# A macaron layer on one core: other holds, another order into the attention, and new homes and order for the output projection

## The chip, the cores and the metric

The kernel runs on 1 core of one Trainium2 chip. The metric is the time of one execution on the device in microseconds (us), lower is better. The engines are named as in the profile: PE (TensorE, matmuls), PEld (its weight loads), ACT (ScalarE), DVE (VectorE), POOL (GpSimd), and SP, whose queue issues all the DMAs spoken of here. Each engine runs its instructions in program order; they wait for each other by semaphores.

## The reference

One layer on x of 1024 tokens by 1024 features, all in float32: a half SwiGLU network, stick-breaking attention with 16 heads of 64, and a second half SwiGLU network with an inner width of 2816.

```
x = x + 0.5 * swiglu(rms_norm(x, g1), w1_in, w1_out)
x = x + attention(rms_norm(x, gm), w_qkv, gq, gk, w_o)
x = x + 0.5 * swiglu(rms_norm(x, g2), w2_in, w2_out)

swiglu(y, w_in, w_out):  gate, up = split(y @ w_in);  (silu(gate) * up) @ w_out
attention:  q, k = rms_norm per head;  z = q k^T / 8;  only keys s < t
            w[t, s] = sigmoid(z[t, s]) * product over s < j < t of (1 - sigmoid(z[t, j]))
            concat(w @ v) @ w_o
```

## The kernel before, in words

Every product is made of three matmuls (L271, L272, L273): an operand is split by `split` (L179: ACT writes a rounded high part; L180: POOL or DVE subtracts it to get the low part), and high x high, low x high and high x low are added up in one PSUM bank. So each operand costs one ACT and one DVE or POOL instruction before PE can use it. In the profile the tiles have the names of the program: `wqh`/`wql` are the parts of the q, k, v weights, `xh`/`xl` those of the normed input, `th`/`tl` those of a turned block of attention weights, `rp` and `u` those of weights on their way into the two networks.

The first network runs to about 672 us. Its second product, `ffn_out`, is made of seven products in the manner of Strassen (`SEVEN`), called m = 5, 1, 4, 3, 7, 2, 6 in this order; each runs over six chunks of the inner width and leaves its result in four banks `ma` or `mb`, which DVE adds to x with a factor of plus or minus a half (L557). A caller's function `at` is called behind chunks, blocks and products, and puts work of the next stage there: sums of squares (L214, ACT), the norm's rates (L188 to L195, many tiny DVE instructions), the scaled rows `xs` (L234, DVE) and their turning on PE into `xh`, `xl`.

The attention goes over eight pairs of heads, p = 0 to 7, one every 67 us, up to 1263 us. In a pair PE makes the scores of blocks (L817, `bz<-kh_s,q_s`), ACT, DVE (a scan, L823) and POOL (a product and a memset, L830 and L828) make the weights `w` from them, PE turns these (L852, `bt<-ident,w`), ACT and DVE split them into `th` and `tl`, and PE applies them to the values (L870, `bo<-th,vst` and `bo<-tl,vst`). Scores alone would leave PE waiting, so the q, k, v product of the next pair (`bq<-wqh,xh`) is cut into steps and laid between. The order is written out in a plan: a pair has parts a, b, c, d with spans (`PARTS`), every step is put at a time of its part (`put`), and the steps are issued sorted by that time. When a row block of q, k, v is finished (L739 to L751), ACT makes squares and copies, DVE the values' low part `vst` (L744), and after four blocks the norm's rates `r` (L751) and `f` (L762), and POOL scales `qk` (L755, L758).

The weights of the pair after next are fetched by `weights_of` in four steps (`LOADS`). So that the ACT conversion (L707) isn't scheduled too early, a tiny POOL instruction first writes one element of each weight tile's place from `qk`: a hold (L706), on which the conversion then depends.

Outputs of pairs are stored to DRAM (L884) and loaded back as rows of `xh` and `xl` (L895). The output projection is in two halves of columns. Its first half's weights are fetched in four pieces `wo0` to `wo3` of two pairs each (L987) and split, the low parts on POOL (`ON_POOL`). Its products for the first seven pairs are laid into the last pair as filler (`SHARES`, 8 places; `project`, L1000 adds to x); the eighth pair's products for all eight row blocks come when the attention has ended. Then the second half runs. `first_weights` fetches the second network's first weights into a ring of 18 tiles `u`, beginning at number 0. All loads and stores stand on SP's one queue, in program order.

Of the kernel before, what the change touches and what calls it, by code (L numbers as in the profile page):

```python
# [34 lines left out]
ON_POOL = {"wo0", "wo1", "wo2", "wo3"}  # L35
# [12 lines left out]
SHARES = (("b", 6.0), ("b", 11.0), ("c", 3.0), ("c", 9.0), ("c", 15.0), ("d", 1.5), ("d", 5.0), ("d", 8.5))  # L48
# [44 lines left out]
SHARE = 7  # L93
# [10 lines left out]
def macaron_kernel(ctx, tc, x, g1, w1_in, w1_out, gm, w_qkv, gq, gk, w_o, g2, w2_in, w2_out, out):  # L104
# [67 lines left out]
    above = cpool.tile([P, 112], F32, name="above")  # L172
# [53 lines left out]
    def norm(pl, row, tbs, gain, ss=None, r=None):  # L226
# [4 lines left out]
        for i, tb in enumerate(tbs):  # L231
            xs = pl["xs"].tile([P, D], F32, name="xs")
            for h in range(2):
                dve.scalar_tensor_tensor(  # L234
                    out=xs[:, HALVES[h]], in0=row(tb, h), scalar=r[:, i : i + 1], in1=gain[:, HALVES[h]],
                    op0=ALU.mult, op1=ALU.mult,
                )
# [97 lines left out]
    def first_weights(pl, raws, behind=None):  # L335

        place["u"] = place["h"] = 0
# [6 lines left out]
    def first_pair(pl, us, turns):  # L344
# [6 lines left out]
        for t, c in ((0, T0), (1, T1)):  # L351
# [14 lines left out]
            for j in range(2):  # L366
                h = small(pl, "h")
                g = pl[f"h{place['h'] + 3}"].tile([P, NHALF], F32, name="h", bufs=1)
# [129 lines left out]
    def ffn_out(pl, w_out, keep, x_from, ahead, at):  # L498
# [25 lines left out]

        open_banks = {}
        loaded = set()
        for m, tag, fresh, goes in SEVEN:
            last = m == SEVEN[-1][0]
            if fresh:
# [18 lines left out]

            n = len(CHUNKS) - BY_BLOCK if last else len(CHUNKS)
            for c in range(n):  # L550
                add(range(4), [c])
                at(x_sb, m, c)
            for t in range(4):
                add([t], range(n, len(CHUNKS)))
                for (th, h), sign in goes:
                    xc = x_sb[h][:, 4 * (1 - th) + t, :]
                    dve.scalar_tensor_tensor(  # L557
                        out=xc, in0=bs[t], scalar=0.5 * sign, in1=xc, op0=ALU.mult, op1=ALU.add
                    )
                if last:  # L560
                    at(x_sb, m, f"block {t}")
            at(x_sb, m, "end")
# [26 lines left out]
    with pools(*RAWS) as pr:  # L589
# [41 lines left out]
        with banks("ps2"), pools(*SECOND) as pl:  # L631
# [4 lines left out]
            def at(x_sb, m, where):  # L636
# [19 lines left out]
                elif (m, where) == (6, 0):  # L656
                    pending.extend(norm(pn, row, (6, 7), gain_m, r=late.pop()))
# [12 lines left out]
            ffn_out(pl | pr, w1_out, keep, x, ops, at)  # L670
# [3 lines left out]

    marks = []
    with ExitStack() as stack:
# [9 lines left out]
        def weights_of(p, state, behind=None):  # L686
# [6 lines left out]
            def step(n, k):  # L693
# [10 lines left out]
                if behind:  # L704
                    there = behind[n]()
# [392 lines left out]
```

## Time and profile before

| what | value |
|---|---|
| time, median of 3 runs | 1969.98 us (1968.36 to 1972.76) |
| the profiled execution's own time | 1967.96 us |
| its span in the trace | 1966.2 us |
| mean granted PE clock | 0.997 |
| busy PE, PEld | 1917.2 us (98%), 1641.7 us (83%) |
| busy DVE, POOL, ACT | 1248.8 us (64%), 1086.9 us (55%), 983.4 us (50%) |
| DMA | 260.25 MB, mean 132 GB/s |

A row of a timeline gives start and duration in us, engine, line, operation, the tiles written and read, and how often; in brackets stands the idle time of the engine just before it and what ended that. Two instructions of a kind in a row can stand in one row with their common time. A row of PE's waits gives the total idle time in us, how often, and the longest. A row of the windows gives for each stretch the busy time of PE, PEld, DVE, ACT and POOL with the count of instructions, then the granted PE clock, the share of DMA time and GB/s.

### The profile page before, as it was taken

What the parts mean: (1) busy time and instruction counts of PE and PEld (TensorE: products, weight loads), DVE (VectorE), ACT (ScalarE), POOL (GpSimd) and SP (SyncE); (2) the same over time, 40 slices, a digit from 0 to 9 for tenths busy, and PEclk for the clock granted to TensorE, in tenths of its full rate; (3) what the DMA queues carried; (4) which work ended last, traced back from release to release, by engine and by line L of the source; (5) the groups of instructions that cost most, each with busy time, mean ns of one, the idle gap of its engine ahead of it and who ended that gap; (6) DMA issues with size and microseconds to landing.
All of it is one profiled execution on the core that took longest, in us unless ns stands there. A gap on an engine that the chain in (4) does not pass through costs nothing.

```text
span 1966.2 us, 27322 instructions
## 1 busy us (share of the span) xinstructions
PE 1917.2 (98%) x9656; PEld 1641.7 (83%) x9656; DVE 1248.8 (64%) x1823; ACT 983.4 (50%) x1802; POOL 1086.9 (55%) x957
## 2 busy tenths in 40 slices
PE   7999999999999899999999999999999999999999
PEld 7978888888888798898889897789888888888887
DVE  7855545536767667877787778474645644547644
ACT  6533433443335467777777776344343343343332
POOL 3667666656445445555655645113666666755454
PEclk9999999999999999999999999999999999999999
DMA  5223323238996311111111234411332332359984
GB/s 209 86 93 122 106 88 120 95 123 287 355 321 222 105 33 44 38 39 44 36 37 42 66 103 164 166 60 54 118 102 100 121 102 86 124 195 350 317 274 148
DMA packets 168504, 260.25 MB, mean 132 GB/s; under 512 B 11568, under 2 KB 81200, under 8 KB 168368
## 3 DMA queue, kind: packets, MB, share of 16 engines
q1 hardware_dynamic: 168368, 258.52, 38.3%
q8 instruction: 75, 1.23, 0.3%
q14 instruction: 61, 0.50, 0.1%
HBM read 198.18 MB, written 60.29 MB: 131 GB/s over the span
## 4 chain that ended last, share of the span: by engine, by line
PE 79%; DVE 9%; POOL 4%; ACT 4%; issue 3%; DMA 1%; SPq 0%; ACTq 0%; DVEq 0%; POOLq 0%
PE ka L271 6%; PE ka L272 6%; PE ka L273 6%; PE kc L273 4%; PE kc L272 4%; PE kc L271 4%; PE kb L272 4%; PE kb L273 4%; PE kb L271 4%; PE bq L271 3%; PE bq L272 3%; PE bq L273 3%; PE ma L271 3%; PE ma L272 3%; PE ma L273 3%
## 5 line engine op out<-in xcount | busy, mean ns | idle before, releaser
L180 POOL TENSOR_TENSOR rp<-raw,rp 128x1024 fp32r<-128x1024 f32 x84 | 205.8, 2453 | 189.7 <-ACT rp L179 174.5
L180 POOL TENSOR_TENSOR u<-sf,u 128x512 fp32r<-128x512 f32 x160 | 225.9, 1413 | 152.3 <-ACT u L179 148.4
L180 POOL TENSOR_TENSOR u<-raw,u 128x512 fp32r<-128x512 f32 x136 | 195.8, 1445 | 173.4 <-ACT u L179 172.4
L830 POOL TENSOR_TENSOR w<-w,om 128x512 f32<-128x512 f32 (+4 forms) x128 | 142.4, 1115 | 120.0 <-DVE om L823 93.6
L179 ACT ACTIVATE u<-sf 128x512 fp32r<-128x512 f32 x160 | 100.7, 630 | 215.3 <-PE kb L272 86.8
L390 DVE TENSOR_TENSOR h<-h 128x512 f32<-128x512 f32 x110 | 135.3, 1235 | 88.6 <-POOL h L494 87.9
L271 PE MATMUL bq<-wqh,xh 128*128 128x384 f32 x512 | 174.6, 341 | 2.1 <-DVE vst L744 2.1
L179 ACT ACTIVATE rp<-rh 128x1024 fp32r<-128x1024 f32 (+1 forms) x78 | 76.5, 984 | 198.4 <-issue 65.4
L273 PE MATMUL bq<-wqh,xl 128*128 128x384 f32 x512 | 172.2, 336 | 0.0
L272 PE MATMUL bq<-wql,xh 128*128 128x384 f32 x512 | 172.1, 336 | 0.0
L271 PE MATMUL ka<-xh,u 128*128 128x512 f32 (+1 forms) x448 | 162.2, 362 | 1.9 <-ACT s L442 1.4
L179 ACT ACTIVATE u<-raw 128x512 fp32r<-128x512 f32 x136 | 85.0, 632 | 154.9 <-PE ka L272 101.3
L272 PE MATMUL ka<-xl,u 128*128 128x512 f32 (+1 forms) x448 | 161.9, 361 | 0.0
L273 PE MATMUL ka<-xh,u 128*128 128x512 f32 (+1 forms) x448 | 161.6, 361 | 0.0
L515 DVE TENSOR_TENSOR raw<-raw 128x1024 f32<-128x1024 f32 (+1 forms) x60 | 86.4, 1445 | 96.4 <-DMA raw<-w_out 76.4
L273 PE MATMUL ma<-rp 128*128 128x512 f32 x352 | 137.6, 391 | 3.6 <-DVE rp L180 3.6
L271 PE MATMUL ma<-rp 128*128 128x512 f32 x352 | 137.9, 392 | 0.1
L272 PE MATMUL ma<-rp 128*128 128x512 f32 x352 | 137.6, 391 | 0.0
L821 ACT ACTIVATE w<-bz,f 128x512 f32<-128x512 f32 (+1 forms) x192 | 112.8, 587 | 46.2 <-PE bz L817 40.6
L494 POOL TENSOR_TENSOR h<-h,g 128x512 f32<-128x512 f32 x80 | 112.5, 1406 | 32.7 <-DVE h L446 32.7
L419 DVE TENSOR_TENSOR sf<-raw 128x512 f32<-128x512 f32 x80 | 80.2, 1003 | 78.0 <-POOL u L180 78.0
L180 DVE TENSOR_TENSOR rp<-rh,rp 128x1024 fp32r<-128x1024 f32 (+1 forms) x70 | 110.0, 1590 | 19.2 <-ACT rp L179 16.7
(253 smaller groups left out, 5550.1 us busy)
## 6 DMA issues: line engine op xcount, KB each, us to landing
raw<-w_out SPq DMA_DIRECT2D x120, 512.0 KB, 5.7
raw<-w_in SPq DMA_DIRECT2D x88, 512.0 KB, 3.5
k<-h SPq DMA_DIRECT2D x154, 256.0 KB, 2.1
rh<-k SPq DMA_DIRECT2D x64, 512.0 KB, 6.0
raw_qkv<-w_qkv SPq DMA_DIRECT2D x64, 192.0 KB, 2.9
x_keep<-x SPq DMA_DIRECT2D x32, 256.0 KB, 2.9
x<-x_keep SPq DMA_DIRECT2D x32, 256.0 KB, 5.0
raw<-w_out SPq DMA_DIRECT2D x24, 256.0 KB, 4.2
```

The lines of the kernel that those rows point to most:

```text
L179: act.activation(hi, raw, AF.Copy)
L180: (engine or dve).tensor_tensor(lo, raw, hi.bitcast(F32), op=ALU.subtract)
L271: pe.matmul(dst, ah, bh, start=start and i == 0, stop=False, skip_group_check=onto)
L272: pe.matmul(dst, ah, bl, start=False, stop=False, skip_group_check=onto)
L273: pe.matmul(dst, al, bh, start=False, stop=stop and i == n - 1, skip_group_check=onto)
L390: dve.tensor_tensor(src, hb[of[0]], hb[of[1]], op=getattr(ALU, of[2]))
L419: dve.tensor_tensor(f[n], x, y, op=op)
L494: pool_e.tensor_tensor(h, h, gs[k], op=ALU.mult)
L515: dve.tensor_tensor(w[0], w[0], w[1], op=getattr(ALU, W_OF[m][2]))
L821: act.activation(to, z, AF.Sigmoid, scale=state["f", half][:, sign, tb % 4, hd : hd + 1])
L830: pool_e.tensor_tensor(wt[:, c1 : c0 + n], wt[:, c1 : c0 + n], om[:, c1 - 1 : c0 + n - 1], op=ALU.mult)
```

## The change

Three parts.

Holds. The hold in front of a weight conversion is now written by an engine and into a part that are named for each step. For the first two of a pair's four steps two DVE instructions write two elements each into the high part, from the rates `r`; the POOL hold from `qk` goes into the low part. For the last two steps POOL writes the high part as before. The first pair's last two steps wait for the last block of `xl`.

The order into the attention. In the first `ffn_out`, the results of m = 2 are no longer added when its products end but by `finish_late`, with a factor that is read from a tile `signs`; that tile is first written from the low part of chunk 2 of m = 6, so everything on it stands behind that split. The norm of rows 6 and 7 gets the same hold on each `xs`.

The output projection. `wo3`'s low part moves from POOL to DVE; the pieces get other rooms; the low parts of `wo0` and `wo1` wait for two notes (`seen`), taken from the last pair's `qk` and `k`, and the high part of `wo2` for the low part of `wo1`. The places of the filler change: row block 6 gets all eight pairs in one go, the eighth pair of row blocks 4 and 5 goes into part d, and row block 7 stands whole at the very end of the attention; four row blocks' eighth pair is left for afterwards. The ring of `u` tiles begins at number 8.

```diff
-ON_POOL = {"wo0", "wo1", "wo2", "wo3"}
+ON_POOL = {"wo0", "wo1", "wo2"}
...
-SHARES = (("b", 6.0), ("b", 11.0), ("c", 3.0), ("c", 9.0), ("c", 15.0), ("d", 1.5), ("d", 5.0), ("d", 8.5))
+SHARES = (
+    (("b", 6.0), 4, (0, 7)), (("b", 11.0), 5, (0, 7)), (("c", 3.0), 0, (0, 7)), (("c", 9.0), 1, (0, 7)),
+    (("c", 15.0), 6, (0, 8)), (("d", 1.5), 2, (0, 7)), (("d", 5.0), 3, (0, 7)), (("d", 8.5), 4, (7, 8)),
+    (("d", 12.5), 5, (7, 8)), (("d", 17.0), 7, (0, 8)),
+)
...
-PROJECTION = ("wa", "x0", "wb", "wc", "we", "wf", "wg", "wd", "wh", "wi", "wj", "wk", "wl", "x1")
-WO_FIRST = ("raw2", "raw3", "raw4", "raw5", "wa", "wb", "wd", "wc")
+PROJECTION = ("wa", "wb", "wc", "wd", "x0", "we", "wf", "wg", "wh", "wi", "wj", "wk", "wl", "x1")
+WO_FIRST = ("raw2", "raw3", "raw4", "raw5", "wa", "wd", "wb", "wc")
...
-    def norm(pl, row, tbs, gain, ss=None, r=None):
+    def norm(pl, row, tbs, gain, ss=None, r=None, behind=None):
...
+            if behind is not None:
+                dve.tensor_scalar(xs[:, 0:1], behind, 1.0, None, op0=ALU.mult)
...
-        place["u"] = place["h"] = 0
+        place["u"], place["h"] = at, at // 2 % H_TILES
...
+        def finish_late(m, goes, result, signs, ops):
+            for i, (_, sign) in enumerate(goes):
+                dve.memset(signs[:, i : i + 1], 0.5 * sign)
+            for t in range(4):
+                result(t, signs)
+            at(x_sb, m, "end", ops)
...
+            late = held is not None and m == SEVEN[-2][0]
...
+            def result(t, scales=None, bs=bs, goes=goes):
+                for i, ((th, h), sign) in enumerate(goes):
+                    xc = x_sb[h][:, 4 * (1 - th) + t, :]
+                    by = 0.5 * sign if scales is None else scales[:, i : i + 1]
+                    dve.scalar_tensor_tensor(out=xc, in0=bs[t], scalar=by, in1=xc, op0=ALU.mult, op1=ALU.add)
+
+            if last and held is not None:
+
+                there = ops[held][1][1][:, 0, 0:1].bitcast(F32)
+                signs = cpool.tile([P, 2], F32, name="signs")
+                dve.tensor_scalar(signs, there.to_broadcast([P, 2]), 1.0, None, op0=ALU.mult)
+                late_result(signs, ops)
...
-                if behind:
-                    there = behind[n]()
-                    pool_e.tensor_tensor(h_[:, k % 4, 0:1], there, there, op=ALU.mult)
+                for engine, to, f in behind[n]:
+                    there = f().to_broadcast([P, 2])
+                    engine.tensor_tensor((h_, l_)[to][:, ks, 0], there, there, op=ALU.mult)
...
-                held = (lambda s=nxt: s["qk", 1][:, 0, 4, 0:1], lambda s=nxt: s["qk", 0][:, 2, 0, 0:1])
+                held = (
+                    ((dve, 0, lambda s=nxt: s["r"][:, 0, 0:1]), (pool_e, 1, lambda s=nxt: s["qk", 1][:, 0, 4, 0:1])),
+                    ((pool_e, 0, lambda s=nxt: s["qk", 0][:, 2, 0, 0:1]),),
+                )
...
+                def note(i, f):
+                    pool_e.tensor_tensor(seen[:, i : i + 1], f(), f(), op=ALU.mult)
+
+                put("c", 14.0, partial(note, 0, lambda s=nxt: s["qk", 1][:, 0, 4, 0:1]))
+                put("d", 1.0, partial(note, 1, lambda s=nxt: s["k", 0, 1][1][:, 0:1].bitcast(F32)))
...
+            if c is HALVES[0] and k < 6:
+
+                there = seen[:, k // 2 : k // 2 + 1] if k < 4 else wo[-1][1][:, 0:1].bitcast(F32)
+                pool_e.tensor_tensor((l_ if k < 4 else h_)[:, 0:1], there, there, op=ALU.mult)
...
-        for i, tb in enumerate(ORDER):
+        for i, (_, tb, pairs) in enumerate(SHARES):
             with as_at(marks[1 + i]):
-                project(tb, range(SHARE), 0, EARLY)
+
+                project(tb, range(*pairs), 0, EARLY if i + 1 < len(SHARES) else ("bt",))
...
-        for tb in ORDER:
-            project(tb, range(SHARE, NP), 0, ROUND)
+        for tb in ORDER[4:]:
+            project(tb, range(NP - 1, NP), 0, ROUND)
...
-        hb = first_pair(pa | pr, first_weights(pa | pr, ahead), {(0, 3): turn_rest})
+        hb = first_pair(pa | pr, first_weights(pa | pr, ahead, at=8), {(0, 3): turn_rest})
```

The change shifts line numbers: L180 becomes L183, L242 is the former L234, L570 the former L557, L783 the former L751, L794 the former L762, L855 the former L823, L908 the former L876, L1047 the former L1000.

DVE in a steady pair, where the rates `r` and `f` of four row blocks are made and a `tl` follows; before:

```order
L823 SCALAR_TENSOR_TENSOR om<-bz,om,first 128x512
L194 TENSOR_TENSOR rs_u<-rs_u,bq 128x16
L195 SCALAR_TENSOR_TENSOR bq<-rs_u,bq 128x16
L751 TENSOR_SCALAR r<-bq 128x4x2
L762 TENSOR_SCALAR f_7945<-bq 128x8 x2
L180 TENSOR_TENSOR tl<-bt,th 128x512
L823 SCALAR_TENSOR_TENSOR om<-bz,first 128x256
```

And now:

```order
L855 SCALAR_TENSOR_TENSOR om<-bz,om,first 128x512
L197 TENSOR_TENSOR rs_u<-rs_u,bq 128x16
L198 SCALAR_TENSOR_TENSOR bq<-rs_u,bq 128x16
L783 TENSOR_SCALAR r<-bq 128x4x2
L794 TENSOR_SCALAR f_7956<-bq 128x8 x2
L738 TENSOR_TENSOR wqh<-r 128x2 x2
L183 TENSOR_TENSOR tl<-bt,th 128x512
L855 SCALAR_TENSOR_TENSOR om<-bz,first 128x256
```

Two holds (L738) stand between the rates and `tl`.

DVE on the way into the attention, in the last products of the first network; `raw` are sums of weights (L515, now L524), `mb` the banks of m = 2; before:

```order
L234 SCALAR_TENSOR_TENSOR xs<-x_4340,rs_y,gain 128x512
L234 SCALAR_TENSOR_TENSOR xs<-x_4341,rs_y,gain 128x512
L515 TENSOR_TENSOR raw<-raw 128x1024 x2
L557 SCALAR_TENSOR_TENSOR x_4340<-mb_5525,x_4340 128x512
L557 SCALAR_TENSOR_TENSOR x_4341<-mb_5525,x_4341 128x512
L557 SCALAR_TENSOR_TENSOR x_4340<-mb_5526,x_4340 128x512
L557 SCALAR_TENSOR_TENSOR x_4341<-mb_5526,x_4341 128x512
L557 SCALAR_TENSOR_TENSOR x_4340<-mb_5527,x_4340 128x512
L557 SCALAR_TENSOR_TENSOR x_4341<-mb_5527,x_4341 128x512
L557 SCALAR_TENSOR_TENSOR x_4340<-mb_5528,x_4340 128x512
L557 SCALAR_TENSOR_TENSOR x_4341<-mb_5528,x_4341 128x512
L180 TENSOR_TENSOR rp<-rh,rp 128x1024
```

And now:

```order
L242 SCALAR_TENSOR_TENSOR xs<-x_4341,rs_y,gain 128x512
L524 TENSOR_TENSOR raw<-raw 128x1024 x2
L183 TENSOR_TENSOR rp<-rh,rp 128x1024
L576 TENSOR_SCALAR signs<-rp 128x2
L240 TENSOR_SCALAR xs<-rp 128x1 x2
L536 MEMSET signs 128x1 x2
L242 SCALAR_TENSOR_TENSOR xs<-x_4340,rs_y,gain 128x512
L570 SCALAR_TENSOR_TENSOR x_4340<-mb_5525,signs,x_4340 128x512
L570 SCALAR_TENSOR_TENSOR x_4341<-mb_5525,signs,x_4341 128x512
L524 TENSOR_TENSOR raw<-raw 128x512
```

The split `rp` comes ahead of the results and of three of the four halves of `xs`, and three small writes stand behind it.

DVE in the last pair, behind the update of the output tile `o1`; `w12`, `w13` and `om` are scans over blocks, `wf` a split of the projection's second half, `x0` the sum with the projection; before:

```order
L780 SCALAR_TENSOR_TENSOR kl_s0_12683<-bz_12684,gk_sb_6223,kh_s0_12682 128x512
L876 TENSOR_TENSOR o1_12678<-bo_12679,o1_12678 64x512
L823 SCALAR_TENSOR_TENSOR w13_12702<-bz_12703,first_6511 128x128
L823 SCALAR_TENSOR_TENSOR om_12718<-bz_12719,first_6511 128x512
L1000 TENSOR_TENSOR x0_13207<-bq_13241,x0_13207 128x512
L823 SCALAR_TENSOR_TENSOR om_12718<-bz_12727,om_12718,first_6511 128x512
```

And now:

```order
L812 SCALAR_TENSOR_TENSOR kl_s0_12706<-bz_12707,gk_sb_6230,kh_s0_12705 128x512
L908 TENSOR_TENSOR o1_12701<-bo_12702,o1_12701 64x512
L183 TENSOR_TENSOR wf_13500<-raw_13497,we_13499 128x1024
L1047 TENSOR_TENSOR x0_13230<-bq_13267,x0_13230 128x512
L855 SCALAR_TENSOR_TENSOR om_12741<-bz_12742,first_6520 128x512
L855 SCALAR_TENSOR_TENSOR w12_12692<-bz_12693,first_6520 128x256
L855 SCALAR_TENSOR_TENSOR w13_12725<-bz_12726,first_6520 128x128
```

The split `wf`, the sum `x0` and the scan `om` now stand ahead of the scans `w12` and `w13`; `w12` stood ahead of `kl_s0` before.

More of the change, by code (lines that the diff above doesn't have):

```diff
@@ L551, in ffn_out @@
                 add(range(4), [c])
-                at(x_sb, m, c)
+                at(x_sb, m, c, ops)
             for t in range(4):
                 add([t], range(n, len(CHUNKS)))
[L555 to L559, printed above, removed]
-                if last:
-                    at(x_sb, m, f"block {t}")
-            at(x_sb, m, "end")
+                if not late:
+                    result(t)
+                if last:
+                    at(x_sb, m, f"block {t}", ops)
+            if late:
+                late_result = partial(finish_late, m, goes, result)
+            else:
+                at(x_sb, m, "end", ops)
     def keeps(name):
```

32 lines of the change are left out of this document (17 added, 15 removed).

## The prediction

> **What bounds the kernel now.** I read the page first, then the list of what TensorE (PE) waits for, then the windows around its longest waits, then the timelines of the other engines at those places.
>
> ```profile
> span 1966.2 us, 27322 instructions
> PE 1917.2 (98%) x9656; PEld 1641.7 (83%) x9656; DVE 1248.8 (64%) x1823; ACT 983.4 (50%) x1802; POOL 1086.9 (55%) x957
> ...
> PE bt L852 <- POOL w L828: 6.2, 8, 1.8
> PE bo L870 <- DVE tl L180: 4.4, 14, 1.2
> PE bo L870 <- ACT th L179: 3.9, 6, 0.7
> PE ma L273 <- DVE rp L180: 3.6, 1, 3.6
> ...
> PE kc L271 <- ACT u L179: 2.3, 1, 2.3
> PE bq L271 <- DVE vst L744: 2.1, 2, 1.2
> PE bt L246 <- DVE xl L180: 1.3, 1, 1.3
> PE kc L273 <- POOL u L180: 0.8, 1, 0.8
> PE bo L271 <- DVE o L876: 0.8, 1, 0.8
> PE bt L271 <- ACT xh L179: 0.5, 1, 0.5
> ```
>
> PE is busy for 1917.2 of 1966.2 us. The change keeps every matmul, so it can win only from the 49 us of idle PE, and from matmuls that run slowly. These rows (total, times, longest) hold 25.9 us of that; most of the rest lies outside the three places that the change touches. The second loss is the clock; the windows give PE busy time first and the granted clock before the DMA share:
>
> ```profile
> 651.30:654.60 3.30, 3.30 (x9) 2.62 (x8) 0.64 (x1) 1.32 (x3) 3.30 (x2) 0.50 0.19 58
> 1190.60:1194.00 3.40, 3.40 (x12) 2.72 (x11) 3.34 (x10) 1.44 (x3) 2.28 (x3) 0.50 0.82 277
> 1330.60:1333.90 3.30, 3.30 (x17) 3.30 (x17) 1.10 (x2) 1.37 (x3) 1.26 (x2) 0.50 0.63 189
> 1131.00:1135.00 4.00, 3.95 (x22) 3.32 (x21) 2.44 (x6) 3.95 (x8) 1.21 (x4) 1.00 0.20 76
> ```
>
> Three stretches of about 3.4 us run at clock 0.50 though PE is always busy: each costs half its length, 1.7 us. Each follows a wait: 3.65, 1.84, and 2.32 with 0.84 us (rows below). A wait of 2.05 us, at 1130, brought none. So a wait of about 2 us costs 1.7 us more in some cases.
>
> The Trainium skill (TensorE: Matmul & The Clock Gate, Part 1: The HAM clock gate) puts the half rate down to an idle window of about 3.4 us in a free-running grid. By that only the wait of 3.65 us could cost clock: part C below would win 3.4 us less, part A would lose 5.1 us less, and the sum would be 1964.2. The trace does not agree, since 1.84 us was followed by 0.50 too, and it decides; on the stretch's length it agrees.
>
> **Part A: the holds in the steady pairs.** Six pairs each have this place (start, duration, then idle time and its end):
>
> ```profile
> 825.39 0.85 ACT L707 ACTIVATE wqh<-raw_qkv 128x768 fp32r<-128x768 f32 x1 [2.05 <-POOL wqh L706]
> 827.49 0.50 PE L870 MATMUL bo<-th,vst 128*128 128x512 f32 x1 [0.64 <-ACT th L179]
> 828.22 0.50 PE L870 MATMUL bo<-tl,vst 128*128 128x512 f32 x1 [0.22 <-DVE tl L180]
> ...
> 822.68 0.69 DVE L180 TENSOR_TENSOR tl<-bt,th 128x512 fp32r<-128x512 f32 x1
> 823.43 0.50 PE L870 MATMUL bo<-tl,vst 128*128 128x512 f32 x1
> 822.17 1.29 POOL L830 TENSOR_TENSOR w<-w,om 128x512 f32<-128x512 f32 x1 [2.11 <-DVE rs_u L194]
> 823.43 1.04 POOL L755 TENSOR_TENSOR qk<-qk,r 128x512 f32<-128x512 f32 x1
> ```
>
> ACT stands 2.05 us before the weight conversion, because POOL writes the hold late; sq, qk, vst and th queue behind it, and PE waits 0.64 + 0.22 = 0.86 us. The new hold comes from DVE, so these 0.86 us go, six times: 5.2 us. Its cost is two DVE instructions of 128x2 ahead of tl at 822.68. That tl ends at 823.37 and PE uses it at 823.43: no slack, so what delays tl delays PE. Such a tiny instruction is cheap or dear by what POOL does at that moment:
>
> ```profile
> 616.05 1.29 POOL L180 TENSOR_TENSOR rp<-raw,rp 128x512 fp32r<-128x512 f32 x1 [0.96 <-ACT rp L179]
> 616.15 1.21 DVE L194 TENSOR_TENSOR rs_u<-rs_u,rs_y 128x2 f32<-128x2 f32 x1
> 617.79 0.16 DVE L194 TENSOR_TENSOR rs_u<-rs_u,rs_y 128x2 f32<-128x2 f32 x1
> ...
> 634.46 2.88 POOL L180 TENSOR_TENSOR rp<-raw,rp 128x1024 fp32r<-128x1024 f32 x1 [0.64 <-ACT rp L179]
> 637.30 2.84 POOL L180 TENSOR_TENSOR rp<-rh,rp 128x1024 fp32r<-128x1024 f32 x1
> 635.00 7.02 DVE L234 SCALAR_TENSOR_TENSOR xs<-x,rs_y,gain 128x512 f32<-128x512 f32 x4
> ```
>
> The same 128x2 operation on SBUF tiles took 0.16 us alone, and 1.21 us when a POOL operation had just begun: it ended with it. The four xs took 7.02 us beside two back-to-back POOL operations, which fits one DVE instruction let in behind each. The hold reads two SBUF operands too, and stands at about 822.7, inside the POOL operation of 822.17 to 823.46. So I take the first hold to end at 823.5 and the second behind the next POOL operation, at 824.6 (823.5 + 1.04). tl then ends at 825.3, and PE, due at 823.43, waits 1.95 us. Per pair 1.95 - 0.86 = 1.09 us lost, 6.5 us in six. A wait of 1.95 us lies between 1.84 (which lost the clock) and 2.05 (which did not): I take it for three of six pairs, 5.1 us. **A: 11.6 us lost.** Bounds: if only the first hold is held up, tl is about 0.9 us late and A is 0; if all six lose the clock, 16.7 us are lost.
>
> The Trainium skill (SBUF — State Buffer, SBUF: two separate sides) says that VectorE with two SBUF inputs and GpSimd share an exclusive lock, held for the whole instruction. The trace agrees (1.21 against 0.16 us). Taking each hold at 0.16 us instead, A would win about 5.2 - 6 x 0.32 = 3.3 us.
>
> **Part B: the order into the attention.**
>
> ```profile
> 644.21 4.86 DVE L557 SCALAR_TENSOR_TENSOR x<-mb,x 128x512 f32<-128x512 f32 x8
> 648.99 1.21 DVE L180 TENSOR_TENSOR rp<-rh,rp 128x1024 fp32r<-128x1024 f32 x1
> 650.26 0.50 PE L273 MATMUL ma<-rp 128*128 128x512 f32 x1 [3.65 <-DVE rp L180]
> ```
>
> The eight results of m=2 (4.86 us) stand ahead of the rp split for which PE waits 3.65 us. They now stand behind it, as do three of the four xs halves. The split can then run at about 642 to 645, and PE is due at 646.6: the wait goes, and its half-clock stretch, 3.65 + 1.7 = 5.35 us. ACT's xh now stands ahead of the third and fourth weight conversions instead of behind them: the xl wait of 1.3 should go, and of the vst waits 2.1, where a longer chain remains, about 1.5. Ideal 8.1 us. Late now are the results and the split of the next chunk, which queue behind the new signs and hold instructions; by the 1.21 us row each of these may sit out a POOL operation. Cost 0 to 5 us, I take 1.6, since by the order some 36 matmuls stand between that split and the next chunk's, 8 us at 0.23 us each. **B: 6.5 us won** (3 to 8.1).
>
> **Part C: output projection and the weights behind it.**
>
> ```profile
> 1129.94 0.39 PE L817 MATMUL bz<-kh_s,q_s 128*128 128x256 f32 x1 [2.05 <-DVE w L823]
> 1186.77 2.36 POOL L180 TENSOR_TENSOR wc<-raw,wd 128x1024 fp32r<-128x1024 f32 x1
> 1189.62 0.33 PE L852 MATMUL bt<-ident,w 128*128 128x128 f32 x1 [1.84 <-POOL w L828]
> 1327.42 1.67 ACT L179 ACTIVATE u<-raw 128x512 fp32r<-128x512 f32 x3 [7.14 <-DVE xs L234]
> 1328.10 0.39 PE L271 MATMUL kc<-xh,u 128*128 128x256 f32 x1 [2.32 <-ACT u L179]
> ```
>
> Won: the wait of 2.05 us falls where SP had just issued a w_o load; that load moves some 40 us back, and I take 1.8. The wait of 1.84 us is for a memset queued on POOL behind the split of 2.36; one such split leaves POOL and the other goes earlier: 1.84 + 1.7 = 3.5. The projection's last block, 24 matmuls of 0.23 us, now covers the end of the attention, where PE waits 0.8 + 0.5: 1.3. With the stream's rooms shifted by eight, ACT converts u tiles some 60 us earlier: 2.32 + 0.84 + 1.7, less 0.5 for the xs behind, 4.4. Together 11.0 us.
>
> Given back: in the last pair, DVE now does the wf split, an x update and om ahead of two scans that stood before them.
>
> ```profile
> 1197.71 0.69 DVE L823 TENSOR_TENSOR_SCAN w<-bz,first 128x256 f32<-128x256 f32 x1
> 1201.55 1.22 DVE L823 TENSOR_TENSOR_SCAN om<-bz,first 128x512 f32<-128x512 f32 x1 [1.47 <-ACT bz L821]
> 1211.59 1.62 DVE L180 TENSOR_TENSOR wf<-raw,we 128x1024 fp32r<-128x1024 f32 x1
> ```
>
> From about 1199.7: wf 1.2 to 1.62, the update 0.7, om 1.22, then the scan 0.69, so the bank behind that scan comes free at about 1203.9, and POOL's products later still; PE, after scores at about 1199.2 and by the order 14 filler matmuls of 0.23 us, is there at about 1202.4. I take 2.5 us (1.2 to 5: ACT's conversion and PE's projection there wait for loads too). The wc split moved onto DVE, 1.2 to 1.62 us amid a close chain: 0.6 (0 to 1.2). The fill in the last part is thinner: each group's transposes, th (0.6), tl (0.69) and apply must cover for each other: 0.7 (0 to 1.5). The two splits held back on POOL (2.4 us each, as the row of 2.36) stand ahead of products that PE takes only some us later: nothing, and about 1.2 us if the loads that wait for their rooms are late. **C: 11.0 - 3.8 = 7.2 us won** (3 to 9.5).
>
> **Sum.** The profiled execution took 1967.96 us (span 1966.2 and 1.8 around it), 2.0 under the median 1969.98 of three runs that span 4.4 us. -11.6 + 6.5 + 7.2 = 2.1 us won: 1965.9, named **1966**; on the median's footing it would be 1968. About 0.2% (3.9 us) is what a measurement of this kernel can tell from no change.
>
> **Rivals.**
> 1. The holds cost little: both slip in behind one POOL operation, A is 0, and the time is 1967.96 - 6.5 - 7.2 = 1954.3. For it: r and f, of the same size, are not stretched in that POOL operation (but they read PSUM). Against: 616.15, and the four xs. Chance 0.27.
> 2. Slower: the lock with POOL strikes wherever a tiny hold stands on DVE. All six pairs wait 1.95 us and lose the clock (A 16.7 lost), and the three instructions of this kind into the attention each sit out a POOL split of 2.4 us: 7.2 late, of which some 3 are slack, so PE waits 4 us at the next chunk and loses 1.7; B is 0.8. Time 1967.96 + 16.7 - 0.8 - 7.2 = 1976.7. It decides from the point where more than about four pairs lose the clock. Chance 0.15.
> 3. The last pair gives C back: loads of o and w_o collide, the wait near 1203 reaches 5 us and the clock goes, C is about 3; time 1970.1. Chance 0.08.
> 4. The waits only move to the next stop on their chains and the change does nothing: 1968. Chance 0.05.
>
> **Chances.** The forecast itself has 0.45; with A between 6.5 and 13 lost and B and C as bounded its own range is 1959 to 1972, which lies on both sides of 3.9 us won: I give 0.18 of it to faster, 0.22 to no change, 0.05 to slower. With the rivals: faster 0.18 + 0.27 + 0.01 = 0.46; the same 0.22 + 0.09 = 0.31; slower 0.05 + 0.15 + 0.03 = 0.23. The range that leaves out two in ten runs from 1951 (rival 1 with B and C near their tops) to 1975 (short of rival 2).
>
> **What would show it.** Right: in each steady pair a DVE hold of 0.8 to 1.2 us, a PE wait of about 2 us for tl where none was, the waits for th gone; clock 0.50 in about three places between 750 and 1100; no wait for rp at 646, for the memset at 1187, for u at 1325; a new wait near 1203. Wrong: holds of 0.16 us in all pairs (then rival 1), or a wait for rp at the next chunk as long as the one removed.

## The result, and the profile after

| kernel | median (lowest to highest), runs | ratio to before, 95% interval |
|---|---|---|
| before | 1969.36 us (1967.66 to 1972.97), 6 | |
| after | 1953.12 us (1951.77 to 1957.07), 6 | 0.9923 [0.9913, 0.9933] |

The change wins 16.2 us, 0.8%. The prediction's sum said 1966, with a range from 1951 to 1975; the time that came is that of its first rival (1954.3). The page of the changed kernel:

```profile
span 1955.3 us, 27335 instructions
PE 1910.4 (98%) x9656; PEld 1638.2 (84%) x9656; DVE 1265.6 (65%) x1839; ACT 986.2 (50%) x1802; POOL 1089.5 (56%) x963
```

PE's waits in it (total, times, longest):

```profile
PE bo L902 <- DVE tl L183: 7.7, 14, 1.2
PE bt L884 <- POOL w L860: 4.7, 8, 0.6
PE ma L280 <- POOL rp L183: 4.4, 2, 2.7
PE ma L281 <- DVE rp L183: 3.3, 1, 3.3
PE bq L279 <- DVE vst L776: 1.9, 2, 1.0
PE bz L849 <- DVE w L855: 1.4, 8, 0.3
```

Gone are the waits for `th` (3.9 before), for `u` (2.3 and 0.8) and the 1.84 us for POOL's memset; that for `xl` fell from 1.3 to 0.3. New are two waits for POOL's `rp`, and `tl` has risen from 4.4 to 7.7. The 3.3 us for DVE's `rp` is not the old one: it stands at 1928, in the second network. The windows at the places of the old slow stretches, and one new one (PE's granted clock stands before the DMA share):

```profile
651.30:654.60 3.30, 2.11 (x10) 1.40 (x8) 3.30 (x6) 3.27 (x8) 1.75 (x1) 1.00 0.55 200
1190.60:1194.00 3.40, 3.26 (x14) 2.10 (x12) 3.22 (x5) 2.33 (x7) 1.29 (x4) 1.00 0.71 217
1330.60:1333.90 3.30, 3.30 (x30) 3.30 (x29) 3.30 (x6) 0.00 (x0) 0.00 (x0) 1.00 0.25 88
1931.20:1934.50 3.30, 3.30 (x8) 2.65 (x9) 1.54 (x2) 0.63 (x1) 1.47 (x1) 0.50 0.00 0
```

All three half-clock stretches of before are gone in this trace, and none stands in the pairs, where the prediction wanted three. (Four later traces with the same order into the attention, e7, e10, e11 and e12, have half clock near 657 again.) The new one, at 1931, follows the new wait of 3.30 us. Another execution of the same kernel (e1_again below, span 1949.6) has neither, so I compare that one with before. Both run the same 9656 matmuls in nearly the same order; the start of the nth in the one trace less its start in the other gives where the time went:

| up to (us in before) | nth start, after less before | step | prediction |
|---|---|---|---|
| 640 | +0.6 | (loads at the start) | |
| 700, behind B | -1.8 | B: 2.4 won | 6.5 won |
| 1120, six pairs | -7.0 | A: 5.2 won | 11.6 lost |
| 1340, behind C | -16.1 | C: 9.2 won | 7.2 won |
| end | -16.6 | | 2.1 won |

### The profile page after: what moved, and what is told of

It is laid out like the page before. It is cut to its first block, busy times and chain, and to the rows that moved or that the text cites. A ratio compares the mean times of both kernels' runs of the same rounds, so it can differ in the third digit from the quotient of the medians.

```text
span 1955.3 us, 27335 instructions
## 1 busy us (share of the span) xinstructions
PE 1910.4 (98%) x9656; PEld 1638.2 (84%) x9656; DVE 1265.6 (65%) x1839; ACT 986.2 (50%) x1802; POOL 1089.5 (56%) x963
## 3 DMA queue, kind: packets, MB, share of 16 engines
q8 instruction: 75, 1.23, 0.3%
## 5 line engine op out<-in xcount | busy, mean ns | idle before, releaser
L183 POOL TENSOR_TENSOR rp<-raw,rp 128x1024 fp32r<-128x1024 f32 x84 | 209.4, 2498 | 190.6 <-ACT rp L182 172.8
L183 POOL TENSOR_TENSOR u<-sf,u 128x512 fp32r<-128x512 f32 x160 | 225.9, 1414 | 151.1 <-ACT u L182 147.2
L183 POOL TENSOR_TENSOR u<-raw,u 128x512 fp32r<-128x512 f32 x136 | 195.8, 1444 | 164.7 <-ACT u L182 163.5
L524 DVE TENSOR_TENSOR raw<-raw 128x1024 f32<-128x1024 f32 (+1 forms) x60 | 94.0, 1569 | 98.2 <-DMA raw<-w_out 92.4
L853 ACT ACTIVATE w<-bz,f 128x512 f32<-128x512 f32 (+2 forms) x192 | 112.3, 585 | 40.5 <-PE bz L849 39.4
L183 DVE TENSOR_TENSOR rp<-rh,rp 128x1024 fp32r<-128x1024 f32 (+1 forms) x70 | 108.4, 1567 | 22.4 <-ACT rp L182 19.7
```

Of the source, the lines that this page charges most:

```text
L183: (engine or dve).tensor_tensor(lo, raw, hi.bitcast(F32), op=ALU.subtract)
L524: dve.tensor_tensor(w[0], w[0], w[1], op=getattr(ALU, W_OF[m][2]))
L853: act.activation(to, z, AF.Sigmoid, scale=state["f", half][:, sign, tb % 4, hd : hd + 1])
```

## The experiments

**e1_again**, the changed kernel once more.

> The changed kernel itself, a second look. Theory: the wait of 3.3 us near the end of the second network (at 1928), with its half-clock stretch, belongs to that one execution and not to the change: this time it is absent and the profiled execution takes about 1952 to 1954 us. Rival: the change brings it every time: it is there again and the profiled execution takes about 1957 us.

1954.07 us (1951.4 to 1956.68, 4 runs), ratio 0.9917 [0.9895, 0.9939]; the profiled execution took 1951.4 and has no wait near 1930. So the 3.3 us belongs to single executions. What decides stands some 40 us ahead of it. The changed kernel's first profile:

```profile
1888.41 2.39 POOL L183 TENSOR_TENSOR rp<-raw,rp 128x1024 fp32r<-128x1024 f32 x1 [0.27 <-ACT rp L182]
...
1888.58 3.30 DVE L524 TENSOR_TENSOR raw<-raw 128x1024 f32<-128x1024 f32 x1 [13.49 <-DMA raw<-w_out]
...
1925.01 4.86 DVE L570 SCALAR_TENSOR_TENSOR x<-mb,x 128x512 f32<-128x512 f32 x8
1929.80 1.21 DVE L183 TENSOR_TENSOR rp<-rh,rp 128x1024 fp32r<-128x1024 f32 x1
...
1931.06 0.79 PE L281 MATMUL ma<-rp 128*128 128x512 f32 x1 [3.30 <-DVE rp L183]
```

The same places in e1_again:

```profile
1887.92 3.08 POOL L183 TENSOR_TENSOR rp<-raw,rp 128x1024 fp32r<-128x1024 f32 x1 [0.27 <-ACT rp L182]
...
1887.36 1.37 DVE L524 TENSOR_TENSOR raw<-raw 128x1024 f32<-128x1024 f32 x1 [12.76 <-DMA raw<-w_out]
...
1918.57 4.86 DVE L570 SCALAR_TENSOR_TENSOR x<-mb,x 128x512 f32<-128x512 f32 x8
1923.36 3.44 DVE L183 TENSOR_TENSOR rp<-rh,rp 128x1024 fp32r<-128x1024 f32 x1
```

DVE's addition waits for a load. Where the load lands 0.17 us after POOL has begun, DVE sits out POOL's operation (3.30 us, not 1.37); where it lands 0.56 us before, POOL waits instead (3.08, not 2.39). Some 35 us on, the eight additions to x stand ahead of a split for which PE then waits. The other traces bear it out: in all five with the long addition at this place (3.16 to 3.36 us: after, e2, e4, e10, e11) PE waits 3.3 us near 1930; in the five with a short one (1.23 to 1.46 us: e1_again, e3, e5, e6, e12) it does not. (e7 to e9 change this place.) How the delay is handed on between the two places is read from the order and not tested by a run. A toss of some tenths of a microsecond decides over 5 to 6 us: executions of one kernel differ by so much from here on, and medians of few runs have to be read with it.

**e2_no_holds**, part A taken back.

```diff
-                    ((dve, 0, lambda s=nxt: s["r"][:, 0, 0:1]), (pool_e, 1, lambda s=nxt: s["qk", 1][:, 0, 4, 0:1])),
+                    ((pool_e, 0, lambda s=nxt: s["qk", 1][:, 0, 4, 0:1]),),
```

> The changed kernel with part A taken back: in the steady pairs the holds come from POOL and go into the high part, as before. Theory (each new hold pair sits out one POOL operation, costs PE 0.8 us, and sheds 1.65 us): the pairs take 66.85 us again instead of 66.0, and the kernel is about 5 us slower than the changed one, about 1958 us. Rival (the prediction's: the holds lose 0 to 12 us): the same or faster than the changed one, 1941 to 1953 us.

1963.41 us (1956.69 to 1965.12, 10 runs), ratio 0.9958 [0.9944, 0.9973]. Against e1_again its matmuls fall back by 5.3 us between 700 and 1120: a pair takes 66.85 us again and not 66.0. The other 4 to 5 us of the medians are not A's in the one execution that has a trace: it has the wait near 1930 (6.4 us with its slow stretches). The ten times lie in two groups, eight at 1962.4 to 1965.1 and two at 1956.7 and 1958.4, which fits a wait that most of them have; no trace shows the other nine. So A wins about 5; that it would lose 11.6 is refuted.

**e4_hold_psum**, the same hold as a DVE operation that reads the rates where they still stand in PSUM (y, the tile from which r is copied).

```diff
+                    if engine is dve:
+                        dve.tensor_scalar((h_, l_)[to][:, ks, 0], there, 1.0, None, op0=ALU.mult)
+                        continue
                     engine.tensor_tensor((h_, l_)[to][:, ks, 0], there, there, op=ALU.mult)
...
-                y = y.rearrange("p (a b) -> p a b", b=4)
+                y = state["y"] = y.rearrange("p (a b) -> p a b", b=4)
...
-                    ((dve, 0, lambda s=nxt: s["r"][:, 0, 0:1]), ...
+                    ((dve, 0, lambda s=nxt: s["y"][:, 0, 0:1]), ...
```

> The changed kernel with the two DVE holds of a steady pair reading the rates where they lie in PSUM, by a scalar multiplication, instead of two operands in SBUF. Theory (the hold is held up by POOL's operation because it reads SBUF on the port that they share): each hold takes about 0.15 us, tl comes 0.8 us earlier, PE's wait of 0.74 us for tl goes in six pairs, and the kernel is about 4 to 5 us faster than the changed one, 1948 to 1949 us. Rival (DVE is held up there by something else, such as the write into the weights' place): the first hold takes 0.85 us again and the time is that of the changed one, 1953 us.

1954.02 us (1953.34 to 1955.21, 4 runs), ratio 0.9918 [0.9898, 0.9937]. The timeline of a pair in the changed kernel:

```profile
819.79 1.29 POOL L862 TENSOR_TENSOR w<-w,om 128x512 f32<-128x512 f32 x1 [2.10 <-DVE rs_u L197]
821.03 1.05 POOL L787 TENSOR_TENSOR qk<-qk,r 128x512 f32<-128x512 f32 x1
...
820.25 0.92 DVE L738 TENSOR_TENSOR wqh<-r 128x2 fp32r<-128x2 f32 x2
821.08 0.68 DVE L183 TENSOR_TENSOR tl<-bt,th 128x512 fp32r<-128x512 f32 x1
...
821.82 0.50 PE L902 MATMUL bo<-tl,vst 128*128 128x512 f32 x1 [0.74 <-DVE tl L183]
```

and the twelve holds of it by duration (ns: least, median, most):

```profile
L738 DVE TENSOR_TENSOR wqh<-r x12: 147/496/862, 754.2 to 1085.0; 128x2 fp32r<-128x2 f32 x12
```

The same place in e4_hold_psum, and its twelve:

```profile
819.16 1.29 POOL L865 TENSOR_TENSOR w<-w,om 128x512 f32<-128x512 f32 x1 [2.10 <-DVE rs_u L197]
...
819.62 0.22 DVE L739 TENSOR_SCALAR wqh<-bq 128x2 fp32r<-128x2 f32 x2
819.76 0.68 DVE L183 TENSOR_TENSOR tl<-bt,th 128x512 fp32r<-128x512 f32 x1
...
820.49 0.50 PE L905 MATMUL bo<-tl,vst 128*128 128x512 f32 x1
```

```profile
L739 DVE TENSOR_SCALAR wqh<-bq x12: 148/150/153, 754.4 to 1080.3; 128x2 fp32r<-128x2 f32 x12
```

With r both holds take 0.92 us and end when POOL's operation ends (819.79 + 1.29 = 821.08); from PSUM they pass in 0.22 us in the middle of the same POOL operation, and PE's wait of 0.74 us is gone. All twelve holds are so. The wait for POOL is what the hold costs: without it the matmuls gain 4.9 us on e1_again between 700 and 1120, six pairs, and a pair takes 65.2 us. Two things changed here, the memory that is read and the operation; e10 below separates them. The median shows nothing of the gain: the profiled execution, the fastest of the four, has the wait near 1930 again and pays 6.4 us there. The other three have no trace, but e9 below keeps the gain to its end.

**e10_hold_one**, the hold reads r in SBUF, but as its one operand.

```diff
+                    if engine is dve:
+                        dve.tensor_scalar((h_, l_)[to][:, ks, 0], there, 1.0, None, op0=ALU.mult)
+                        continue
                     engine.tensor_tensor((h_, l_)[to][:, ks, 0], there, there, op=ALU.mult)
```

> The changed kernel with VectorE's two holds as operations with one operand in on-chip memory (a copy of r times 1) and not as a product of two such operands. Theory 1 (what waits for GpSimd is an operation with two operands in SBUF): the first hold takes 0.15 us and not 0.85, the waits of 0.74 us for tl are gone, a pair takes 65.2 us and not 66.0, as with the hold that reads PSUM. Theory 2 (any VectorE operation on SBUF waits for GpSimd's): 0.85 us as before, a pair takes 66.0 us. By the time: 1948 to 1950 against 1953 when the wait near 1930 does not occur, 6 us more when it does.

1955.35 us (1952.13 to 1958.63, 4 runs), ratio 0.9919 [0.9894, 0.9943]. In its timeline:

```profile
821.65 0.93 DVE L739 TENSOR_SCALAR wqh<-r 128x2 fp32r<-128x2 f32 x2
...
823.22 0.50 PE L905 MATMUL bo<-tl,vst 128*128 128x512 f32 x1 [0.72 <-DVE tl L183]
```

Theory 1 falls: one operand in SBUF waits like two, in all six pairs (850 to 861 ns for the first hold). So it is the memory, and not the number of operands. The Trainium skill (SBUF — State Buffer, SBUF: two separate sides) counts among those that take the lock also VectorE operations in a two-port mode, and names the fp32 copy from SBUF to SBUF as one. The trace agrees with that: 0.93 us from SBUF, 0.22 us from PSUM; but the hold is a multiplication by 1 and not that copy, and no run here shows in which mode it ran.

**e3_no_late**, part B taken back, and **e5_no_late_pad**, the same with 32 bytes kept.

```diff
-                    there = ops[2][1][1][:, 0, 0:1].bitcast(F32)
-                    pending.extend(norm(pn, row, (6, 7), gain_m, r=late.pop(), behind=there))
+                    pending.extend(norm(pn, row, (6, 7), gain_m, r=late.pop()))
...
-            ffn_out(pl | pr, w1_out, keep, x, ops, at, held=2)
+            ffn_out(pl | pr, w1_out, keep, x, ops, at)
...
-        for f in weights_of(0, states[0], ((), last_x)):
+        for f in weights_of(0, states[0], ((), ())):
```

> The changed kernel with part B taken back: the results of m = 2 and the norm of rows 6 and 7 where they were, and no hold on the first pair's last weights. Theory (the wait of 3.65 us and its half clock were swapped for two waits of 2.7 and 1.7 us, and 1 us more came from xl): about 1.5 us slower than the changed one, 1954.5 us. Rival (part B wins the 6.5 us of the prediction and part C less than it seems): about 6 us slower, 1959 to 1960 us.

1970.45 us (1968.7 to 1974.97, 10 runs), ratio 1.0009 [0.9996, 1.0022]: 16 us lost, far outside both theories, and most of it where the edit does not reach. By the starts of the matmuls, against e1_again 7.2 us are lost evenly from 140 to 455 us and 8.4 from 1340 to 1735, without a wait and at full clock: a matmul of `ffn_in` starts every 231.9 ns there and not 226.7. The edit drops the tile `signs`, 32 bytes in the pool at the bottom of SBUF, so most of the buffers above it move down by 32 bytes: in the built program the rooms of `u` begin at byte 93344 = 64 x 1458.5 and not at 93376 = 64 x 1459. `xh` and `xl` lie below it and stay. e5 takes the same code and adds

```diff
+    pad = cpool.tile([P, 2], F32, name="pad")
+    pool_e.memset(pad, 0.0)
```

> The order into the attention taken back as in the run that lost 16 us, but with 32 bytes of on-chip memory kept in the place of the small tile that the late results use, so that every tile behind it lies where it lies in the changed kernel. Theory 1 (the address): the ffn_in matmuls of that run started 231.9 ns apart on average and not 226.7, because every buffer lay 32 bytes lower; with the pad they start 226.7 ns apart again, and what is left is the order's own worth, about 2.5 us by the two traces between 640 and 700 us: 1955 to 1957. Theory 2 (the order itself makes the loss): still 1968 to 1972. Theory 3 (the prediction's step: the order is worth 6.5 us): 1959 to 1961.

1955.49 us (1952.84 to 1958.22, 4 runs), ratio 0.9932 [0.9914, 0.995]. The windows of e3, then those of e5 (the count behind PE's busy time is the matmuls):

```profile
140.00:440.00 300.00, 300.00 (x1296) 242.64 (x1295) 147.32 (x160) 117.28 (x200) 194.94 (x139) 1.00 0.31 104
1780.00:1900.00 120.00, 120.00 (x531) 99.38 (x530) 81.38 (x74) 45.28 (x48) 61.06 (x25) 1.00 0.92 326
```

```profile
140.00:440.00 300.00, 300.00 (x1325) 248.42 (x1324) 154.30 (x161) 117.91 (x203) 194.93 (x140) 1.00 0.32 107
...
651.90:655.20 3.30, 3.30 (x10) 2.55 (x9) 0.41 (x1) 1.32 (x3) 3.30 (x2) 0.53 0.13 38
```

300 us hold 1296 matmuls in e3 and 1325 in e5; before has 1325 too. So the address cost 7.2 + 8.4 = 15.6 us: shown by the pad, for between the two lie only the 32 bytes and one memset of them. It is one pair of addresses, and no general rule. In `ffn_in` matmuls of `u` with `xh`, which did not move, and with sums such as `t3h`, which did, both got slower; in `ffn_out`, where both operands moved, the 120 us hold 531 in both. Why only `ffn_in` suffers stays open. What is left is B's own worth: e5 loses 2.0 us to e1_again from 646 to 700. But that is one execution against one, and e1_again is among the best there: e7 and e10, which have B, lose 1.8 us to it in the same stretch. e5 has the wait for the split and the half clock behind it (the last row above), as before had:

```profile
650.62 0.50 PE L281 MATMUL ma<-rp 128*128 128x512 f32 x1 [3.64 <-DVE rp L183]
```

**e6_late_squares**: where B gave its gain back. The trace of after behind the split that is now early:

```profile
646.47 0.17 DVE L576 TENSOR_SCALAR signs<-rp 128x2 f32<-128x2 f32 x1
649.31 3.38 DVE L570 SCALAR_TENSOR_TENSOR x<-mb,signs,x 128x512 f32<-128x512 f32 x5
...
648.17 0.63 ACT L217 ACTIVATE hs<-x 128x512 f32<-128x512 f32 x1 [5.61 <-DVE x L570]
650.78 1.05 ACT L182 ACTIVATE rp<-rh 128x1024 fp32r<-128x1024 f32 x1
...
652.85 3.19 POOL L183 TENSOR_TENSOR rp<-raw,rp 128x1024 fp32r<-128x1024 f32 x1 [7.50 <-ACT rp L182]
...
656.10 0.50 PE L280 MATMUL ma<-rp 128*128 128x512 f32 x1 [2.69 <-POOL rp L183]
659.47 0.50 PE L280 MATMUL ma<-rp 128*128 128x512 f32 x1 [1.72 <-POOL rp L183]
```

The late results make ACT's squares late (5.61 us idle), the squares stand ahead of the conversion of chunk 4, POOL gets that late, and PE waits 2.69 and 1.72 us. So the squares were put behind the conversions:

```diff
                 elif (m, where) == (2, "end"):
+                    act.activation(half[:, :, 0], ops[5][0][0][:, 0, 0:4].bitcast(F32), AF.Copy)
                     squares(pn, row, range(4), half, (0,))
```

> The changed kernel with ScalarE's two squares of the late results standing behind its conversions of the last two chunks (one more tiny copy on ScalarE holds them). Theory 1: the new waits of 2.69 and 1.72 us at the last ffn_out operands of the first feed-forward come from ScalarE's squares standing ahead of the conversions; they shrink to under 1 us together, and the time falls by 3 to 4.5 us, to about 1949.5. Theory 2: GpSimd's split is late for its own reasons (the lock, the operand's load): the waits stay, no change within 1 us.

1956.5 us (1955.24 to 1958.5, 4 runs), ratio 0.9941 [0.9924, 0.9957]: no gain. POOL's waits are gone, and the next ones stand there:

```profile
652.72 3.37 DVE L570 SCALAR_TENSOR_TENSOR x<-mb,signs,x 128x512 f32<-128x512 f32 x5
656.01 1.21 DVE L183 TENSOR_TENSOR rp<-rh,rp 128x1024 fp32r<-128x1024 f32 x1
...
657.27 0.50 PE L281 MATMUL ma<-rp 128*128 128x512 f32 x1 [3.21 <-DVE rp L183]
```

DVE's own split of chunk 4 stands behind the late additions. Near 671 a wait of 3.43 us for `xs` comes on top, with a half-clock stretch behind it: 3.9 us lost against e1_again. So theory 1 named a chain that was there, and its forecast failed: the other chain alone is enough to keep PE waiting.

**e7_second_held**, late results in the second network too.

```diff
-        ffn_out(pl | pr, w2_out, keep, x_keep[1], ops, at)
+        ffn_out(pl | pr, w2_out, keep, x_keep[1], ops, at, held=2)
```

> The changed kernel with the late results used in the second feed-forward's output too: there the eight additions of the seventh product stand behind the split of the third chunk of the next one. Theory 1: the wait of 3.30 us with the half-clock stretch near 1930, which some executions have, comes from those eight additions (4.86 us) standing ahead of that split when GpSimd and VectorE meet in the wrong order; it is gone in every execution: median 1950 to 1951.5, no run above 1953. Theory 2: the split is late for its load or for GpSimd: runs still scatter from 1951.5 to 1957, or the wait moves to the end: up to 1955.

1951.94 us (1951.32 to 1953.06, 4 runs), ratio 0.9915 [0.99, 0.993]. No wait near 1930 in the trace, and no run above 1953.1: nearer to theory 1, though the median is 0.4 us above its range and the slowest run 0.06 us above its bound. That run is the profiled one, and it loses 1.8 us from 646 to 680 that e1_again did not. Its trace alone does not test the edit, for DVE's addition came first there (1.45 us), and without the edit too there would have been no wait; e9 below is the test.

**e8_all_in** (the edits of e4, e6 and e7) and **e9_psum_held** (those of e4 and e7).

> Three edits on the changed kernel: VectorE's hold reads PSUM, ScalarE's squares stand later, late results in the second feed-forward too. If the three are each worth what the traces show (5 us by the pairs, 3.8 us by the squares, 2 to 5 us by the wait near 1930) and none gives it back: 1941 to 1944. If the gain in the pairs is given back at the next fixed point (the load of the weights, the wait near 1930): 1947 to 1951.

> Two edits on the changed kernel: VectorE's hold reads PSUM, and the late results in the second feed-forward too; ScalarE's squares stay where they are. Theory 1: the two do not touch each other; the pairs give 4.1 to 4.4 us more and the wait near 1930 with its half-clock stretch (6.2 us when it occurs) is gone in every execution: median 1946.5 to 1948.5, no run above 1950. Theory 2 (as with the squares moved too): the gain is given back at another place: 1950 to 1952.

e8: 1950.6 us (1948.74 to 1950.99, 4 runs), 0.9905 [0.9891, 0.992]. e9: 1947.22 us (1946.65 to 1950.56, 4 runs), 0.9886 [0.9866, 0.9907]. e8 comes out as its second case, e9 as its theory 1. e9 beats both kernels, by 22.6 us against before on the same chip; e8 is the poorer by e6's edit (4.8 us behind e1_again at 680, e9 1.0). e9 has the gain of e4 in its trace and keeps it to the end (3.8 us ahead of e1_again from 1120 on). Its DVE lost the toss near 1884, and PE still does not wait near 1920: the additions stand behind the split there:

```profile
1884.26 3.29 DVE L524 TENSOR_TENSOR raw<-raw 128x1024 f32<-128x1024 f32 x1 [13.50 <-DMA raw<-w_out]
...
1920.68 1.21 DVE L183 TENSOR_TENSOR rp<-rh,rp 128x1024 fp32r<-128x1024 f32 x1
1921.93 0.17 DVE L576 TENSOR_SCALAR signs<-rp 128x2 f32<-128x2 f32 x1
1922.34 2.07 DVE L570 SCALAR_TENSOR_TENSOR x<-mb,signs,x 128x512 f32<-128x512 f32 x3
```

One of its four runs (1950.56) exceeds what was expected; it has no trace.

**e11_ring0**, the ring of `u` begins at 0 again, and **e12_old_homes**, the homes are those of before.

```diff
-        hb = first_pair(pa | pr, first_weights(pa | pr, ahead, at=8), {(0, 3): turn_rest})
+        hb = first_pair(pa | pr, first_weights(pa | pr, ahead), {(0, 3): turn_rest})
```

> The changed kernel with the second feed-forward's first weights back at the first homes of the ring (places 0 and not 8). Theory 1 (the prediction's term): PE waits again near 1310 for the weights u, with a half-clock stretch, 4.5 us: 1957 to 1959. Theory 2 (the new order of the output projection has freed those homes earlier too): no wait, within 1 us of 1953.

```diff
-PROJECTION = ("wa", "wb", "wc", "wd", "x0", "we", "wf", "wg", "wh", ...
+PROJECTION = ("wa", "x0", "wb", "wc", "we", "wf", "wg", "wd", "wh", ...
```

> The changed kernel with the homes of the output projection's tiles as they were (x0 again between wa and wb, so that it lies on rooms of the ring of u); the ring begins at 8 and the order of the filler is the new one. Theory 1 (the homes, not the ring's beginning, removed the wait for u): late conversions of u stand behind the last rows again, PE waits near 1310 for u, 2 to 4.5 us; and the loads of w_o go out late again, so a wait of about 2 us near 1120 and some around 1180 may come back: 1956 to 1962. Theory 2 (the new order of the filler removed it): no wait for u, and only what the last pair loses, 1953 to 1956.

e11: 1954.44 us (1952.27 to 1958.01, 4 runs), 0.9921 [0.9899, 0.9943]; no wait for `u`, and less than 0.1 us lost against e1_again from 1270 to 1700, so theory 2, though the median is 1.4 us above its 1953 (the trace has the wait near 1930). e12: 1954.98 us (1954.26 to 1955.52, 4 runs), 0.9928 [0.9911, 0.9945]; its timeline:

```profile
1315.48 1.67 ACT L182 ACTIVATE u<-raw 128x512 fp32r<-128x512 f32 x3 [7.06 <-DVE xs L242]
...
1310.35 0.38 PE L281 MATMUL kc<-xh,u 128*128 128x256 f32 x1 [1.97 <-POOL u L183]
1314.27 1.56 PE L254 MATMUL kb<-ident,xs 128*128 128x128 f32 x9 [1.02 <-DVE xs L242]
```

This is the picture of before: three conversions of `u` behind `xs`, ACT idle for 7.06 us, and 4.4 us lost against e1_again from 1300 to 1320. So the homes make this term, and the ring's beginning nothing. The median lies below theory 1's 1956: the wait came as it said, the losses near 1120 and 1180 did not. The loads of w_o, which the expectation put late too, cost nothing in e12: near 1176 it is 1.3 us better than e1_again.

## Why the prediction was wrong in its sum, point by point

**A failed, and it is nearly the whole error** (11.6 lost against 5.2 won). Three terms of it:
- "the second behind the next POOL operation, at 824.6" did not happen. The first hold sat out POOL's operation, as said; the second passed right behind it, 0.02 us before POOL's next one (821.01 against 821.03), in 0.15 us; so it is in all six pairs, 844 to 862 ns and then 147 to 149 (the second starting 0.01 to 0.02 us ahead of POOL each time). The row on which the step rested, the four `xs` in 7.02 us, has operations of 0.7 us; that tiny ones queue in the same way was a guess and had its own rival, which is how it came out. PE's wait for `tl` is 0.74 us and not 1.95.
- The clock: 5.1 us were set for three of six pairs; with waits of 0.74 us no pair has a stretch at 0.50.
- The gain was too small: the idle 0.64 and 0.22 us that go are worth 0.89 and 0.41 by the starts of the matmuls, and three more of 0.1 each go along. A wait is counted from the modelled end of a matmul of 0.39 to 0.50 us, while the next would start 0.23 us after it. Per pair 1.65 us won and 0.79 lost.

The rival's figure, A = 0, was 5 us too low as well; that its time agrees to 1.2 us is luck, since B's shortfall takes back most of what A gives. That the measured time lies in the forecast's range is owed to that rival: the range was drawn to take it in, while A, the term that made the sum's size, went the other way.

**B was mis-sized** (6.5 against 2.4 in e1_again). The wait of 3.65 us and its slow stretch went, as said: 5.5 us by the starts, and the `xl` wait gave 1.0. Two terms failed. The first is "I take 1.6" for what queues behind the late results: it costs 4.3 by the starts, from 656 to 660. The prediction named the split of the next chunk; what stood in the trace was ACT's squares ahead of its conversion, and behind these, as e6 showed, that split too. The second is the `vst` waits, 1.5 in the prediction and 0.2 by the starts. The feared hold instructions cost it nothing in the first profile (`signs` 0.17 us); in e1_again `signs` sat out a POOL operation for 2.24 us, and PE's waits there were no longer. The 2.4 is at the upper end: from 640 to 700 the nine traces with this order win 0.5 (e7) to 2.5 us (e2) against before, 2.0 in the middle, the two without it (e3, e5) -0.07 and 0.35. The three lowest, e7, e10 and e12, have two half-clock steps at 657 again.

**C was about right in size** (7.2 against 9.2; 8.9 to 9.5 in the other traces that leave C and the addresses alone), with one wrong reason. What each place gives is read from the starts; a run took back only the homes and the ring's beginning. The starts give: the wait near 1130 2.25 (1.8 predicted), the memset with its clock 2.7 (3.5), the end of the attention 1.4 (1.3), `u` 4.5 (4.4). Given back near 1203 1.5 (2.5), and at the wc split 1.5 (0.6), since it meets POOL as well:

```profile
1173.18 2.60 DVE L183 TENSOR_TENSOR wc<-raw,wb 128x1024 fp32r<-128x1024 f32 x1 [0.76 <-ACT wb L182]
```

The thinner fill cost nothing (0.7 predicted): 1.3 us more were won from 1205 to 1245. "With the stream's rooms shifted by eight" is refuted by e11; by e12 it is the homes of the projection's tiles. That it is x0's, which lay on the rooms 2 to 7 of `u` and now lies on none, is likely and not shown alone, since e12 moves wb, wc and wd along.

## What to carry to other kernels

Before pricing a tiny instruction that waits on another engine, ask which memory it reads: the same hold cost 0.92 us from SBUF and 0.22 us from PSUM beside a busy POOL (two holds each time). Where DVE's order is free, put what PE waits for ahead of what only has to be done some time; in e9 that removed a wait that only some executions have. But look at what then comes late: in B it cost 4.3 us. After any edit that adds or drops a small tile, compare the addresses of the big buffers before believing the time.

## What the runs showed of the hardware that was not expected

- 32 bytes of address: matmuls 231.9 ns apart and not 226.7 in `ffn_in` with `u` at an odd multiple of 32 bytes, no difference in `ffn_out` (e3, e5).
- Two tiny DVE operations behind each other pass together behind one POOL operation: 0.85 and 0.15 us.
- Which engine goes first is a toss of some tenths of a microsecond, and the loser waits until the other is done: the same `signs` took 0.17 and 2.24 us in two executions of one kernel.
- Half clock goes by a grid. In each of the fourteen traces all half-clock stretches begin on one grid of 3.413 us: those of before, at 651.26, 1190.56 and 1330.51, lie 158 and 41 steps apart. What counts is how long PE is idle inside the one step ahead, and not how long a wait is. From 40 us on, up to the last matmuls, all sixteen steps at full clock with 1.83 to 3.30 us of idle PE were followed by half clock; of those with less (1.76 us at most) only one was, 1.60 us near 1205 in e3. So the limit lies somewhere about 1.6 to 1.83 us here, about half a step. Idle time is counted from modelled ends. A step of before with half clock behind it (3.41 - 1.57 = 1.84 us idle), and one of e1_again with none (1.76):

```profile
1187.15:1190.56 3.41, 1.57 (x15) 1.37 (x14) 2.94 (x9) 2.83 (x7) 3.41 (x6) 1.00 0.90 282
654.97:658.38 3.41, 1.65 (x6) 1.05 (x6) 3.01 (x2) 0.84 (x1) 3.41 (x3) 1.00 0.57 158
```

This explains what the prediction could only call "some cases": before's wait of 1.84 us lies inside one step, and its wait of 2.05 us near 1130 is cut by a grid point (1.47 and 0.82 us idle in its two steps). It also makes executions differ: 2.04 and 1.72 us of idle PE near 657 brought no slow stretch in e1_again, 2.40 and 1.39 us at the same place brought two steps of it, 6.8 us, in e12. The waits of up to 0.76 us in the pairs brought none in any trace.
